# Near and strided values of a dilated head summed in the same two PSUM banks

## The chip, the cores and the metric

The kernel runs on one core of a Trainium2 chip. The metric is the device time of one execution in microseconds (us). The kernel before takes 1144.44 us as the median of 3 runs (1144.17 to 1147.55). Five engines take part: TensorE (PE in the profile; its weight loads are PEld), VectorE (DVE), ScalarE (ACT), GpSimd (POOL), and SyncE (SP), which issues the DMAs. Each engine runs its own instructions in order.

## The reference

Two layers of a decoder on 1024 tokens of width 1024, each with a pre-RMSNorm, a gate and a residual. Layer 1 is a latent attention that this change does not touch. Layer 0 has 8 sliding-window heads (A) and 8 dilated heads (B). A dilated head of 64 columns attends three times, with window and stride (128, 1), (512, 4) and (2048, 16); the three outputs are merged by the weights of their softmax denominators:

```python
for window, dil in B_CONFIGS:                      # (128,1), (512,4), (2048,16)
    bias_b, band_b = band_bias(rel_bias[:, A_HEADS:], dil, window // dil)
    o, lse = banded_attention(to_strided(qb, dil), to_strided(kb, dil), to_strided(vb, dil), bias_b, band_b)
    outs.append(from_strided(o, b, s, dil))
    lses.append(from_strided(lse, b, s, dil))
wts = jax.nn.softmax(jnp.stack(lses), axis=0)
ob = jnp.sum(wts[..., None] * jnp.stack(outs).astype(jnp.float32), axis=0)
...
return (o * jax.nn.silu(z)) @ w_out
```

## The kernel before, in words

Layer 0 makes the normed input transposed (`hH`, `hL`: a rounded part and the rest, since each product is made of reduced-precision matmuls), projects values, queries, keys and gates with `tproj`, runs 16 heads in 8 pairs (pairs 0 to 3 are dilated, 4 to 7 sliding), multiplies by the gate and projects out.

A projection (`tproj`, L144) gives 128 columns (a pair of heads) by 1024 tokens in two halves of 512 tokens; 24 matmuls of 512 columns make a half, and an evacuation takes the half out of its bank.

A dilated head (`head_b`, L530) has two sets of scores. The near scores (`banded`, L238) take 8 blocks of 128 queries against their own and the previous block of keys, in 4 parts; the strided scores (`s4`, L554) take the tokens of each residue mod 4 (the stride 16 is folded into the bias of the stride 4). `scores` (L216) runs two matmuls a region into a bank `sc` (two of them), DVE adds the bias and takes the row minimum (L227), ACT takes the exponential (L230). Keys lie by residue (the token 4j + r at r*256 + j). Queries lie in token order in `q`; a copy by residue, `q4`, is made by POOL after the second half of the projection (L470) and feeds the strided scores only.

The two sets have row statistics in different row orders; `to_tokens`, `merge` and `from_tokens` (L571 to L608) bring them together by small matmuls (L578, L604) with permutation matrices and give each row its factor, `fac`.

The values: POOL scales the rows of the score tiles (`scale_rows`, L235), PE transposes four 128 by 128 pieces into a bank, ACT and DVE take them out as `pth` and `ptl` (`transpose_split`, L183), and matmuls add values times these into banks tagged `ot`, of which there are two (L201). The near values (`banded_pv`, L254) go to two such banks in token order, key block by key block: two matmuls of up to 256 query columns for each. Each bank is taken out by `evac_sum` (L105): an ACT copy of one half of the partitions, a DVE add of the other (L108), into the tile `o`. Then the strided values (`pv4`, `pv4b`) take two banks again, in the order of residues; four DVE adds of 64 by 512 elements (L655) read them and add them into `o` at every fourth place:

```python
O4 = d["O"].rearrange("p (i r) -> p r i", r=4)
...
for half in (acc[g].ps[0:HD], acc[g].ps[HD:P]):
    V.tensor_tensor(dst, dst, half.rearrange("p (r i) -> p r i", r=2), op=ALU.add)
```

`finish` (L484) multiplies the gate by `o` on POOL and sends it to memory.

The order: the loop at L703 emits, for each head n, its near values beside the next head's scores, then its strided values beside the next head's statistics, then a projection to fill (queries and keys of the next pair after an even head, the pair's gate after an odd one). The kernel is built with a planner (`schedule_with_timeline_sim=True`) that simulates a timeline and sets each engine's order from it, so projections stand between the steps of the heads in the trace.

Of the kernel before, what the change touches and what calls it, by code (L numbers as in the profile page):

```python
# [10 lines left out]
F32 = mybir.dt.float32  # L11
F32R = mybir.dt.float32r
# [3 lines left out]
ALU = mybir.AluOpType  # L16
AX = mybir.AxisListType
# [3 lines left out]
SEQ = 1024  # L21
# [19 lines left out]
def f(ap):  # L41
    return ap.bitcast(F32)
# [152 lines left out]
class Acc:  # L195
# [2 lines left out]
        self.c, self.ps, self.first, self.parts = c, c.bank("ot", parts), None, parts  # L198

    def add(self, cols, lhsT, rhs, stop=False):  # L200
        m = self.c.mark = self.c.T.matmul(self.ps[:min(self.parts, lhsT.shape[-1]), cols], lhsT, rhs,  # L201
                                          start=self.first is None, stop=stop, skip_group_check=True)
        if self.first is None:
            self.first = m
        else:
            self.c.order(self.first, m)
# [83 lines left out]
def layer0(c, x, norm_w, rel_bias, w_in, w_out, onehot, band, perm, x1d, tables, before_out, x1_done):  # L290
# [86 lines left out]
    def tl(pool, shape, dt, tag, bufs):  # L377
        return pool.tile(shape, dt, name=tag, tag=tag, bufs=bufs)
# [1 line left out]
    pm = sp.tile([P, 4 * P + 312], F32, name="pm")  # L380
    dma.dma_start(pm, perm)

    S4, S4T = pm[:, P:2 * P], pm[:, 3 * P:4 * P]
    o = 4 * P
    in4, out4, sel, unsel = [pm[:, o + a:o + b] for a, b in ((8, 12), (20, 24), (24 + 128, 24 + 192), (24 + 192 + 64, 24 + 192 + 96))]

    def bias_tile(h, cfg, tag):
        b = tl(sp, [P, 256], F32, tag, 2)
        dma.dma_start(b, bass.AP(wr.tensor, wr.offset + (cfg * 16 + h) * P * 384 + 127, [[383, P], [1, 256]]))
        return b  # L390

    def q_evac(Qe, Qo):
        def evac(hf, ps, s):
            c.copy(Qe[0:HD, s], ps[0:HD], 0.125)
            c.copy(Qo[HD:P, s], ps[HD:P], 0.125)
            c.low(Qe[HD:P, s], ps[0:HD], Qe[0:HD, s], 0.125)
            c.low(Qo[0:HD, s], ps[HD:P], Qo[HD:P, s], 0.125)
# [54 lines left out]
    def proj_qk(pr):  # L452
        e = pairs[pr]
        b = pr < 4

        def alloc():
            e["q"] = [tl(qk, [P, SEQ], F32R, "q1", 3) for _ in range(2)]
            if b:
                e["q4"] = [tl(qk, [P, SEQ], F32R, "q4", 2) for _ in range(2)]
                e["k"] = [tl(qk, [P, SEQ], F32R, "kh", 3) for _ in range(2)]  # L460
                e["kl"] = [tl(qk, [P, SEQ], F32R, "kl", 3) for _ in range(2)]
            else:
                e["k"], e["kl"] = [A["k"][(pr - 4) // 2]] * 2, [A["kl"][(pr - 4) // 2]] * 2
        ev_k = lambda hf, ps, s: k_evac(*e["k"], *e["kl"], True)(hf, ps, s)

        def ev_q(hf, ps, s):
            q_evac(*e["q"])(hf, ps, s)
            if b and hf:
                for a, t in zip(e["q"], e["q4"]):
                    G.tensor_copy(t.rearrange("p (r j) -> p r j", r=R4), f(a).rearrange("p (j r) -> p r j", r=R4))  # L470
        out = [alloc]
        if b:
            out += tproj(c, hH, hL, w_in, B_COLS[1] + pr * P, ev_k) + [lambda: (dup(*e["k"]), dup(*e["kl"]))]
        return out + tproj(c, hH, hL, w_in, (B_COLS[0] + pr * P) if b else (pr - 4) * P, ev_q)
# [9 lines left out]
    def finish(pr):  # L484
        e = pairs[pr]
        eng = G if pr < 7 else V
        for hf in range(2):
            s = slice(hf * HALF, (hf + 1) * HALF)
            eng.tensor_tensor(e["gate"][:, s], e["gate"][:, s], e["o"][:, s], op=ALU.mult)
            if pr == 7:  # L490
                gH, gL = e["split"]
                c.copy(gH[:, s], e["gate"][:, s])
                c.low(gL[:, s], e["gate"][:, s], gH[:, s])
        if pr < 7:
            dma.dma_start(gd[pr], e["gate"])
# [34 lines left out]
    def head_b(pr, ei):  # L530
# [3 lines left out]
        p1, p4 = [], []  # L534

        def begin():
            nat = bias_tile(8 + h, 0, "b1")

            b1 = tl(sp, [P, 256], F32, "b1r", 2)
            G.tensor_copy(b1.rearrange("p (k r a) -> p k r a", k=2, r=R4), nat.rearrange("p (k a r) -> p k r a", k=2, r=R4))  # L540
            d["b4"] = bias_tile(8 + h, 1, "b4")

            N, L = d["nat"], d["own"] = tl(sp, [P, 2, 2, 8], F32, "nat", 2), tl(sp, [P, 2, 8], F32, "own", 2)
            k, kl = [e[n][ei].rearrange("p (r j) -> p r j", r=R4) for n in ("k", "kl")]
            d["t4"] = [e["q4"][ei].rearrange("p (r j) -> p r j", r=R4), k, kl]

            def keys(a, b):
                if b - a == 1:
                    return [t[:, :, a * RA:b * RA] for t in (k, kl)]
                return [e[n][ei].rearrange("p (r n a) -> p n r a", r=R4, a=RA)[:, a:b] for n in ("k", "kl")]  # L550
            d["parts"] = banded(c, p1, e["q"][ei], keys, b1, N[:, 0, 0], N[:, 0, 1], BIG)
            d["parts"][0]()

        def s4(r):  # L554
# [11 lines left out]
        def spread(out, vals, mask, vb, mb):  # L566

            shape = list(out.shape)
            V.tensor_tensor(out, vals.unsqueeze(vb).to_broadcast(shape), mask.unsqueeze(mb).to_broadcast(shape), op=ALU.mult)

        def to_tokens():  # L571
            N, L = d["nat"], d["own"]
            u = tl(sp, [P, 64], F32, "u", 1)
            for vh in range(4):
                spread(u[:, 16 * vh:16 + 16 * vh].rearrange("p (b r) -> p b r", r=4),
                       L.rearrange("p v (h r) -> p (v h) r", r=4)[:, vh], in4, 1, 2)
            ps = c.bank("pt")
# [21 lines left out]
        def from_tokens():  # L599
            fac, e = d["fac"], d["e"]  # L600
            u = tl(sp, [P, 64], F32, "u", 1)[:, :32]
            spread(u.rearrange("p (b r) -> p b r", r=4), e[:, 1], out4, 2, 1)
            ps = c.bank("pt")
            T.matmul(ps[:, 0:32], S4T, u, start=True, stop=True)  # L604
            x = tl(sp, [P, 64], F32, "x", 1)[:, :32]
            V.tensor_tensor(x, ps[:, 0:32], unsel, op=ALU.mult)
            V.tensor_reduce(fac[:, 1].rearrange("p (h r) -> p h r", h=2), x.rearrange("p (h b r) -> p h r b", h=2, r=4),
                            axis=AX.X, op=ALU.add)  # L608
# [11 lines left out]
            dma.dma_start(f(V4).rearrange("p (a b) d -> p a b d", b=2),  # L620
                          bass.AP(vd.tensor, vd.offset + h * P, [[4 * R_, P], [R_, 4], [HALF * R_, 2], [1, P]]))

        def evac(hf, acc):
            if hf == 0:
                d["O"] = out_rows(pr, lo)
            c.evac_sum(d["O"][:, hf * HALF:(hf + 1) * HALF], acc, lo)
        pv1 = banded_pv(c, p1, lambda: d["fac"][:, 0], lambda k: d["v"][0][:, k], evac)
        fc = lambda j: d["fac"][:, 1, j:j + 1]
        acc = []

        def pv4(g):
            if g == 0:
                acc.extend([Acc(c, P), Acc(c, P)])
            sl = []
            for r in (2 * g, 2 * g + 1):
                scale_rows(c, p4[r][:, 0:P], fc(r))
                scale_rows(c, p4[r][:, P:384], fc(4 + r))
                sl += [p4[r][:, 0:P], p4[r][:, P:256]]
            ph, pl = transpose_split(c, sl)
            for i in range(2):  # L640
                s = 2 * (2 * g + i)
                cc = slice(i * 256, (i + 1) * 256)
                pv2(acc[g], cc, d["v"][1][:, s], ph, pl, cc)

        def pv4b():
            O4 = d["O"].rearrange("p (i r) -> p r i", r=4)
            ph, pl = transpose_split(c, [p4[r][:, 256:384] for r in range(4)])
            for g in range(2):
                for i in range(2):
                    r = 2 * g + i  # L650
                    pv2(acc[g], slice(i * 256 + P, (i + 1) * 256), d["v"][1][:, 2 * r + 1], ph, pl,
                        slice(r * P, (r + 1) * P), i == 1)
                dst = O4[:, 2 * g:2 * g + 2]
                for half in (acc[g].ps[0:HD], acc[g].ps[HD:P]):
                    V.tensor_tensor(dst, dst, half.rearrange("p (r i) -> p r i", r=2), op=ALU.add)  # L655
# [717 lines left out]
```

## Time and profile before

| | |
|---|---|
| median of 3 runs | 1144.44 us |
| profiled execution | 1145.62 us, span 1143.8 us |
| busy over the span: PE, PEld | 1082.5 us (95%), 924.3 us (81%) |
| DVE, ACT, POOL | 695.2 us (61%), 589.4 us (52%), 504.5 us (44%) |
| mean granted TensorE clock | 0.974 of full speed |
| matmuls of L201 (both inputs) | 864 |
| POOL copies of q (L470) | 8, median 2034 ns |

Busy times are unions of the instructions' durations. A matmul's row has its latency, so the time that matmuls cost in a stream is read from start to start. PEclk is the granted clock as a share of 2.4 GHz; 0.50 is the lower level of 1.2 GHz. The name after `<-` in brackets is what ended the idle time before an instruction.

### The profile page before, as it was taken

How to read it: one execution, taken by the hardware profiler on the slowest of the kernel's cores; microseconds unless marked ns; L12 is line 12 of the kernel's file. 1: busy time of each engine (PE TensorE's matmuls, PEld its weight loads, DVE VectorE, ACT ScalarE, POOL GpSimd, SP SyncE). 2: the span in 40 equal slices, each digit the busy share in tenths (PEclk: the TensorE clock that was granted, in tenths of full speed). 3: DMA queues.
4: the chain of work that ended last, by engine and by line, in shares of the span. 5: the costliest groups of instructions: out<-in, count | busy, mean ns of one | idle time of the engine just before them, and what ended most of it. 6: DMA issues, size and time to landing. Idle time of an engine off the chain costs nothing.

```text
span 1143.8 us, 17221 instructions
## 1 busy us (share of the span) xinstructions
PE 1082.5 (95%) x5862; PEld 924.3 (81%) x5862; DVE 695.2 (61%) x1675; ACT 589.4 (52%) x1419; POOL 504.5 (44%) x535
## 2 busy tenths in 40 slices
PE   7998989899989999999999999999999999988997
PEld 4786778788878888778889988779888888777786
DVE  6534777557776665663331242678888898885333
ACT  5425545455555565653223232567777777685211
POOL 3113545445354344563113123275755665676301
PEclk9999989899999899989999999999999999999999
DMA  9948115142223221164322011132302311620312
GB/s 303 279 142 167 51 47 138 43 116 75 74 85 102 78 83 60 36 193 145 106 76 66 10 47 47 46 79 66 75 14 66 70 31 40 175 74 19 111 74 74
DMA packets 85975, 102.42 MB, mean 90 GB/s; under 512 B 6832, under 2 KB 69840, under 8 KB 85888
## 3 DMA queue, kind: packets, MB, share of 16 engines
q1 hardware_dynamic: 85888, 101.33, 31.6%
q8 instruction: 46, 0.75, 0.3%
q14 instruction: 41, 0.34, 0.1%
HBM read 67.97 MB, written 21.28 MB: 78 GB/s over the span
## 4 chain that ended last, share of the span: by engine, by line
PE 79%; DVE 8%; ACT 4%; DMA 4%; issue 3%; POOL 1%; SPq 0%; POOLq 0%; ACTq 0%; DVEq 0%
PE tp L116 14%; PE tp L118 14%; PE tp L117 14%; PE ot L201 8%; PE pt L188 7%; PE sc L1077 3%; PE sc L1078 2%; PE sc L1079 2%; PE ot L118 2%; PE sc L223 2%; PE ot L116 2%; PE ot L117 2%; PE sc L224 2%; PE pt L116 1%; PE pt L118 1%
## 5 line engine op out<-in xcount | busy, mean ns | idle before, releaser
L235 POOL TENSOR_TENSOR pc<-pc,ast 128x896 f32<-128x896 f32 (+7 forms) x128 | 145.6, 1155 | 114.6 <-DVE ast L1090 104.6
L116 PE MATMUL tp<-hH,wh 128*128 128x512 f32 x480 | 191.7, 400 | 0.6 <-ACT hH L96 0.3
L117 PE MATMUL tp<-hL,wh 128*128 128x512 f32 x480 | 190.5, 397 | 0.0
L118 PE MATMUL tp<-hH,wl 128*128 128x512 f32 x480 | 190.3, 397 | 0.0
L101 DVE TENSOR_TENSOR ptl<-pt,pth 128x512 fp32r<-128x512 f32 (+2 forms) x248 | 157.7, 643 | 40.2 <-ACT pth L96 36.1
L96 ACT ACTIVATE pth<-pt 128x512 fp32r<-128x512 f32 (+2 forms) x248 | 135.9, 562 | 75.3 <-PE pt L188 71.3
L111 POOL TENSOR_TENSOR wl<-wst,wh 128x512 fp32r<-128x512 f32 x60 | 78.3, 1309 | 146.6 <-ACT wh L96 124.8
L201 PE MATMUL ot<-pth,vt 128*128 128x256 f32 (+3 forms) x432 | 128.7, 313 | 12.4 <-ACT pth L96 5.1
L201 PE MATMUL ot<-ptl,vt 128*128 128x256 f32 (+3 forms) x432 | 116.8, 305 | 7.2 <-DVE ptl L101 6.9
L1088 ACT ACTIVATE pc<-sc,ast 128x896 f32<-128x896 f32 (+7 forms) x128 | 94.8, 741 | 28.9 <-DVE ast L1086 21.8
L116 PEld LDWEIGHTS tp<-hH,wh 128*128 128x128 f32 x480 | 91.5, 191 | 18.2 <-DVE kl L101 0.7
L118 PEld LDWEIGHTS tp<-hH,wl 128*128 128x128 f32 x480 | 91.3, 190 | 17.7
L1086 DVE CUSTOM_DVE_ANT_0 sc<-sc,mask 128x256 f32<-128x256 f32 (+7 forms) x128 | 97.3, 761 | 12.7 <-PE sc L1079 6.8
L117 PEld LDWEIGHTS tp<-hL,wh 128*128 128x128 f32 x480 | 91.4, 190 | 16.6
L201 PEld LDWEIGHTS ot<-pth,vt 128*128 128x128 f32 x432 | 83.6, 196 | 25.0 <-ACT pth L96 9.6
L188 PE MATMUL pt<-ident,pc 128*128 128x128 f32 x576 | 89.8, 277 | 1.0 <-POOL pc L235 0.9
L201 PEld LDWEIGHTS ot<-ptl,vt 128*128 128x128 f32 (+1 forms) x432 | 75.6, 179 | 17.3 <-DVE ptl L101 12.4
L235 POOL TENSOR_TENSOR p<-p,fac 128x256 f32<-128x256 f32 (+1 forms) x128 | 65.4, 549 | 48.1 <-DVE e L597 45.3
L1077 PE MATMUL sc<-kh,qh 96*128 96x384 f32 (+4 forms) x192 | 72.9, 380 | 4.6 <-ACT pc L1088 3.5
L188 PEld LDWEIGHTS pt<-ident,pc 128*128 128x128 f32 x576 | 68.2, 142 | 7.2 <-POOL pc L235 1.4
L96 ACT ACTIVATE wh<-wst 128x512 fp32r<-128x512 f32 x60 | 37.9, 632 | 58.3 <-PE tp L117 39.1
L1078 PE MATMUL sc<-kl,qh 96*128 96x384 f32 (+4 forms) x192 | 66.2, 345 | 1.7 <-DMA kl<-kd 1.7
(319 smaller groups left out, 2518.4 us busy)
## 6 DMA issues: line engine op xcount, KB each, us to landing
wst<-in_ab_w_in_dram SPq DMA_DIRECT2D x44, 256.0 KB, 3.1
kh<-kh SPq DMA_DIRECT2D x17, 256.0 KB, 3.1
kl<-kl SPq DMA_DIRECT2D x17, 256.0 KB, 4.2
xt<-in_x_dram SPq DMA_DIRECT2D x8, 512.0 KB, 5.8
vd<-vt SPq DMA_DIRECT2D x8, 512.0 KB, 3.8
vt<-vd SPq DMA_DIRECT2D x32, 128.0 KB, 3.1
vt<-vd SPq DMA_DIRECT2D x8, 512.0 KB, 5.0
xr<-in_x_dram SPq DMA_DIRECT2D x8, 512.0 KB, 4.0
```

The costliest lines, as they stand in the source:

```text
L96: return self.S.activation(out, in_, AF.Copy, scale=scale)
L101: return self.V.tensor_tensor(out, in_, f(high), op=ALU.subtract)
L116: m = self.order(after, self.order(prev, self.T.matmul(ps, lh, rh, start=start, stop=False)))
L117: m = self.order(m, self.T.matmul(ps, lh, rl, start=False, stop=False))
L118: return self.order(m, self.T.matmul(ps, ll, rh, start=False, stop=stop))
L188: c.T.transpose(ps[:, i * P:(i + 1) * P], s, c.ident)
L201: m = self.c.mark = self.c.T.matmul(self.ps[:min(self.parts, lhsT.shape[-1]), cols], lhsT, rhs, start=self.first is None, stop=stop, skip_ ...
L235: c.scaled = c.G.tensor_tensor(ap, ap, factor.to_broadcast(list(ap.shape)), op=ALU.mult)
L1077: m = c.order(m, T.matmul(o, qh[0:96, q], kh[0:96, k0:k1], start=True, stop=False))
L1078: m = c.order(m, T.matmul(o, qh[0:96, q], kl[0:96, k0:k1], start=False, stop=False))
L1086: V.tensor_tensor_reduce(out=ps, in0=ps, in1=mask[:, SEQ - n:], scale=-1.0, scalar=BIG, op0=ALU.add, op1=ALU.min, accum_out=neg)
L1088: S.activation(pt, ps, AF.Exp, bias=neg, scale=-1.0, accum_out=den)
```

## The change

The queries are evacuated by residue straight from PSUM into `q`, which now feeds the strided scores. POOL makes from it, after each half, the near queries `qn`: within each block of 128 tokens, by residue mod 4 and then by place (32 each). So rows of near scores stand in that order, the same one in which the near keys already were. The bias table of the near scores is loaded in four DMAs of 32 rows. The maps between the two row orders become one matrix, `same`. The near values are written by four matmuls a key block, each with an output of two runs (two residues, 64 or 32 columns each), into the two `ot` banks that the strided values then add to; these are taken out once, by `evac_sum`, at the end. `o` of a dilated pair lies by residue, and `finish` reads it and the gate accordingly.

```diff
+    def add_to(self, out, lhsT, rhs, stop=False):
+        m = self.c.mark = self.c.T.matmul(out, lhsT, rhs, start=self.first is None, stop=stop, skip_group_check=True)
...
-    S4, S4T = pm[:, P:2 * P], pm[:, 3 * P:4 * P]
+    same = sp.tile([P, R4, RA], F32, name="same")
+    V.tensor_reduce(same[:, 0], c.ident.rearrange("p (b a) -> p a b", a=RA), axis=AX.X, op=ALU.add)
+    V.tensor_copy(same[:, 1:], same[:, 0:1].to_broadcast([P, R4 - 1, RA]))
...
-    def bias_tile(h, cfg, tag):
+    def bias_tile(h, cfg, tag, quarters=False):
...
+        if quarters:
+            for r in range(R4):
+                dma.dma_start(b[r * RA:(r + 1) * RA], bass.AP(wr.tensor, o + 383 * r, [[4 * 383, RA], [1, 256]]))
...
-    def q_evac(Qe, Qo):
+    def q_evac(Qe, Qo, strided):
...
+            if strided:
+                e, o = [t.rearrange("p (r h j) -> p h r j", r=R4, h=2)[:, hf] for t in (Qe, Qo)]
+                ps = ps.rearrange("p (j r) -> p r j", r=R4)
...
-            q_evac(*e["q"])(hf, ps, s)
-            if b and hf:
-                for a, t in zip(e["q"], e["q4"]):
-                    G.tensor_copy(t.rearrange("p (r j) -> p r j", r=R4), f(a).rearrange("p (j r) -> p r j", r=R4))
+            q_evac(*e["q"], b)(hf, ps, s)
+            if b:
+                for a, t in zip(e["q"], e["qn"]):
+                    G.tensor_copy(t.rearrange("p (b r a) -> p r b a", r=R4, a=RA)[:, :, 4 * hf:4 * hf + 4],
+                                  f(a).rearrange("p (r b a) -> p r b a", r=R4, a=RA)[:, :, 4 * hf:4 * hf + 4])
...
+            if pr < 4:
+                g = e["gate"][:, s].rearrange("p (j r) -> p r j", r=R4)
+                eng.tensor_tensor(g, g, e["o"].rearrange("p (r h j) -> p h r j", r=R4, h=2)[:, hf], op=ALU.mult)
...
-            nat = bias_tile(8 + h, 0, "b1")
+            nat = bias_tile(8 + h, 0, "b1", True)
...
-            d["t4"] = [e["q4"][ei].rearrange("p (r j) -> p r j", r=R4), k, kl]
+            d["t4"] = [e["q"][ei].rearrange("p (r j) -> p r j", r=R4), k, kl]
...
-            d["parts"] = banded(c, p1, e["q"][ei], keys, b1, N[:, 0, 0], N[:, 0, 1], BIG)
+            d["parts"] = banded(c, p1, e["qn"][ei], keys, b1, N[:, 0, 0], N[:, 0, 1], BIG)
...
-            T.matmul(ps[:, 0:64], S4, u, start=True, stop=True)
+            T.matmul(ps[:, 0:64], same, u, start=True, stop=True)
...
-            T.matmul(ps[:, 0:32], S4T, u, start=True, stop=True)
+            T.matmul(ps[:, 0:32], same, u, start=True, stop=True)
...
-        def evac(hf, acc):
-            if hf == 0:
-                d["O"] = out_rows(pr, lo)
-            c.evac_sum(d["O"][:, hf * HALF:(hf + 1) * HALF], acc, lo)
-        pv1 = banded_pv(c, p1, lambda: d["fac"][:, 0], lambda k: d["v"][0][:, k], evac)
+        def near(b0, n, v, ph, pl, at):
+            for w, t in ((v, ph), (v[:, :HD], pl)):
+                t = t[:, at:at + n * P].rearrange("p (b r a) -> p r b a", b=n, r=R4)
+                for g in range(2):
+                    o = acc[g].ps.rearrange("p (r j) -> p r j", r=2)[:, :, b0 * RA:(b0 + n) * RA]
+                    acc[g].add_to(o[:w.shape[-1]], w, t[:, 2 * g:2 * g + 2])
...
+        def pv1(i):
+            k = 2 * i
+            if i == 0:
+                acc.extend([Acc(c, P), Acc(c, P)])
+                scale1(0)
+            for b in (k + 1, k + 2):
+                if b < NT:
+                    scale1(b)
+            ph, pl = transpose_split(c, [blk(k, k), blk(k + 1, k), blk(k + 1, k + 1)] + ([blk(k + 2, k + 1)] if k + 2 < NT else []))
+            v = d["v"][0]
+            near(k, 2, v[:, k], ph, pl, 0)
+            near(k + 1, 2 if k + 2 < NT else 1, v[:, k + 1], ph, pl, 256)
...
         def pv4(g):
-            if g == 0:
-                acc.extend([Acc(c, P), Acc(c, P)])
...
         def pv4b():
-            O4 = d["O"].rearrange("p (i r) -> p r i", r=4)
             ph, pl = transpose_split(c, [p4[r][:, 256:384] for r in range(4)])
+            O = out_rows(pr, lo)
             for g in range(2):
...
-                dst = O4[:, 2 * g:2 * g + 2]
-                for half in (acc[g].ps[0:HD], acc[g].ps[HD:P]):
-                    V.tensor_tensor(dst, dst, half.rearrange("p (r i) -> p r i", r=2), op=ALU.add)
+                c.evac_sum(O[:, g * HALF:(g + 1) * HALF], acc[g].ps, lo)
```

## Rows read from the trace of the kernel before

**Rows 1.** windows of the stage: length, busy us (x instructions) of PE, PEld, DVE, ACT, POOL; granted clock; DMA

```profile
130.00:150.00 20.00, 12.96 (x77) 11.24 (x77) 19.54 (x59) 11.56 (x41) 8.30 (x10) 0.82 0.29 80
...
200.00:214.00 14.00, 9.86 (x59) 8.47 (x58) 10.29 (x23) 4.95 (x12) 12.29 (x16) 0.90 0.31 81
...
214.00:320.00 106.00, 105.54 (x605) 91.56 (x605) 69.75 (x213) 56.31 (x168) 48.01 (x67) 0.98 0.28 73
...
380.00:400.00 20.00, 17.18 (x104) 15.67 (x103) 14.42 (x33) 12.48 (x36) 7.53 (x9) 0.83 0.29 86
```

**Rows 2.** windows again, three stretches at half the clock, same columns

```profile
146.30:156.50 10.20, 7.90 (x36) 7.63 (x37) 8.75 (x29) 5.98 (x23) 8.14 (x17) 0.50 0.17 46
211.20:217.90 6.70, 5.84 (x19) 4.85 (x19) 3.69 (x10) 2.42 (x9) 1.28 (x1) 0.50 0.01 2
388.70:395.40 6.70, 6.30 (x34) 6.12 (x32) 5.59 (x17) 4.71 (x14) 2.52 (x2) 0.50 0.30 103
```

**Rows 3.** groups by line and form, 84 to 400 us: busy, mean ns, idle before

```profile
L655 DVE TENSOR_TENSOR o<-o,ot 64x512 f32<-64x512 f32 x32 | 34.0, 1086 | 5.7 <-PE ot L201 5.1
...
L108 DVE TENSOR_TENSOR o<-ot,o 64x512 f32<-64x512 f32 x18 | 12.3, 685 | 4.6 <-ACT o L96 4.3
...
L103 DVE SCALAR_TENSOR_TENSOR q<-tp,q 64x512 fp32r<-64x512 f32 x24 | 16.5, 689 | 20.1 <-ACT q L96 19.7
...
L101 DVE TENSOR_TENSOR kl<-tp,kh 64x512 fp32r<-64x512 f32 x16 | 11.0, 687 | 7.5 <-ACT kh L96 7.2
...
L96 ACT ACTIVATE o<-ot 64x512 f32<-64x512 f32 x19 | 11.2, 592 | 13.2 <-PE ot L201 12.7
```

**Rows 4.** timeline of PE, place A: start, us, instruction, [idle before, releaser]

```profile
147.01 0.48 PE L223 MATMUL sc<-kh,q 128*128 128x128 f32 x1 [2.18 <-ACT p L230]
...
149.83 0.61 PE L604 MATMUL pt<-u,pm 128*128 128x32 f32 x2 [1.59 <-DVE u L569]
```

**Rows 5.** timeline of DVE, place A, same columns

```profile
143.39 2.06 DVE L655 TENSOR_TENSOR o<-o,ot 64x512 f32<-64x512 f32 x2
...
147.44 1.07 DVE L655 TENSOR_TENSOR o<-o,ot 64x512 f32<-64x512 f32 x1
```

**Rows 6.** timeline of all engines, place B

```profile
203.32 3.76 POOL L235 TENSOR_TENSOR p<-p,fac 128x128 f32<-128x128 f32 x8
...
206.66 1.08 DVE L655 TENSOR_TENSOR o<-o,ot 64x512 f32<-64x512 f32 x1
...
207.77 1.41 DVE L103 SCALAR_TENSOR_TENSOR q<-tp,q 64x512 fp32r<-64x512 f32 x2
...
208.52 3.97 POOL L470 CAST q<-q 128x1024 fp32r<-128x1024 f32 x2 [0.20 <-DVE q L103]
...
208.60 0.36 PE L223 MATMUL sc<-kh,q 128*128 128x256 f32 x1 [1.70 <-DVE q L103]
...
209.73 2.05 DVE L655 TENSOR_TENSOR o<-o,ot 64x512 f32<-64x512 f32 x2
...
211.93 0.44 PE L201 MATMUL ot<-pth,vt 128*128 128x128 f32 x1 [0.68 <-DVE o L655]
```

**Rows 7.** timeline of PE, place C

```profile
387.88 0.36 PE L201 MATMUL ot<-pth,vt 128*128 128x256 f32 x1 [1.78 <-DVE o L655]
388.07 0.28 PE L201 MATMUL ot<-ptl,vt 128*128 128x256 f32 x1
388.19 0.28 PE L201 MATMUL ot<-pth,vt 128*128 128x256 f32 x1
```

**Rows 8.** timeline of PE, the last strided values of a head

```profile
384.15 0.27 PE L201 MATMUL ot<-pth,vt 128*128 128x128 f32 x1
...
384.50 0.23 PE L201 MATMUL ot<-ptl,vt 128*64 128x128 f32 x1
```

**Rows 9.** groups by line and form, POOL, 84 to 400 us

```profile
L489 POOL TENSOR_TENSOR gate<-gate,o 128x512 f32<-128x512 f32 x8 | 10.1, 1288 | 7.2 <-DVE o L655 7.2
```

**Rows 10.** one line's instructions, the bias tables: ns min/median/max, first and last start

```profile
L389 SPq DMA_DIRECT2D b<-wr x24: 319/339/731, 47.0 to 443.6; - x24
```

More of the change, by code (lines that the diff above doesn't have):

```diff
@@ L200, in add @@
     def add(self, cols, lhsT, rhs, stop=False):
-        m = self.c.mark = self.c.T.matmul(self.ps[:min(self.parts, lhsT.shape[-1]), cols], lhsT, rhs,
-                                          start=self.first is None, stop=stop, skip_group_check=True)
+        self.add_to(self.ps[:min(self.parts, lhsT.shape[-1]), cols], lhsT, rhs, stop)
+    def add_to(self, out, lhsT, rhs, stop=False):
+        m = self.c.mark = self.c.T.matmul(out, lhsT, rhs, start=self.first is None, stop=stop, skip_group_check=True)
         if self.first is None:
@@ L381, in layer0 @@
     dma.dma_start(pm, perm)
-    S4, S4T = pm[:, P:2 * P], pm[:, 3 * P:4 * P]
     o = 4 * P
-    in4, out4, sel, unsel = [pm[:, o + a:o + b] for a, b in ((8, 12), (20, 24), (24 + 128, 24 + 192), (24 + 192 + 64, 24 + 192 + 96))]
-    def bias_tile(h, cfg, tag):
-        b = tl(sp, [P, 256], F32, tag, 2)
-        dma.dma_start(b, bass.AP(wr.tensor, wr.offset + (cfg * 16 + h) * P * 384 + 127, [[383, P], [1, 256]]))
+    quarter, unsel = pm[:, o + 8:o + 12], pm[:, o + 24 + 192 + 64:o + 24 + 192 + 96]
+    same = sp.tile([P, R4, RA], F32, name="same")
+    V.tensor_reduce(same[:, 0], c.ident.rearrange("p (b a) -> p a b", a=RA), axis=AX.X, op=ALU.add)
+    V.tensor_copy(same[:, 1:], same[:, 0:1].to_broadcast([P, R4 - 1, RA]))
+    same = same.rearrange("p r a -> p (r a)")
+    def bias_tile(h, cfg, tag, quarters=False):
+        b = tl(sp, [P, 256], F32, tag, 2)
+        o = wr.offset + (cfg * 16 + h) * P * 384 + 127
+        if quarters:
+            for r in range(R4):
+                dma.dma_start(b[r * RA:(r + 1) * RA], bass.AP(wr.tensor, o + 383 * r, [[4 * 383, RA], [1, 256]]))
+        else:
+            dma.dma_start(b, bass.AP(wr.tensor, o, [[383, P], [1, 256]]))
         return b
-    def q_evac(Qe, Qo):
+    def q_evac(Qe, Qo, strided):
         def evac(hf, ps, s):
[L394 to L397, printed above, removed]
+            e, o = Qe[:, s], Qo[:, s]
+            if strided:
+                e, o = [t.rearrange("p (r h j) -> p h r j", r=R4, h=2)[:, hf] for t in (Qe, Qo)]
+                ps = ps.rearrange("p (j r) -> p r j", r=R4)
+            c.copy(e[0:HD], ps[0:HD], 0.125)
+            c.copy(o[HD:P], ps[HD:P], 0.125)
+            c.low(e[HD:P], ps[0:HD], e[0:HD], 0.125)
+            c.low(o[0:HD], ps[HD:P], o[HD:P], 0.125)
         return evac
@@ L458, in alloc @@
             if b:
-                e["q4"] = [tl(qk, [P, SEQ], F32R, "q4", 2) for _ in range(2)]
+                e["qn"] = [tl(qk, [P, SEQ], F32R, "qn", 2) for _ in range(2)]
                 e["k"] = [tl(qk, [P, SEQ], F32R, "kh", 3) for _ in range(2)]
@@ L488, in finish @@
             s = slice(hf * HALF, (hf + 1) * HALF)
-            eng.tensor_tensor(e["gate"][:, s], e["gate"][:, s], e["o"][:, s], op=ALU.mult)
+            if pr < 4:
+                g = e["gate"][:, s].rearrange("p (j r) -> p r j", r=R4)
+                eng.tensor_tensor(g, g, e["o"].rearrange("p (r h j) -> p h r j", r=R4, h=2)[:, hf], op=ALU.mult)
+            else:
+                eng.tensor_tensor(e["gate"][:, s], e["gate"][:, s], e["o"][:, s], op=ALU.mult)
             if pr == 7:
@@ L575, in to_tokens @@
                 spread(u[:, 16 * vh:16 + 16 * vh].rearrange("p (b r) -> p b r", r=4),
-                       L.rearrange("p v (h r) -> p (v h) r", r=4)[:, vh], in4, 1, 2)
+                       L.rearrange("p v (h r) -> p (v h) r", r=4)[:, vh], quarter, 1, 2)
             ps = c.bank("pt")
-            T.matmul(ps[:, 0:64], S4, u, start=True, stop=True)
-            x = tl(sp, [P, 64], F32, "x", 1)
-            V.tensor_tensor(x, ps[:, 0:64], sel, op=ALU.mult)
-            V.tensor_reduce(N[:, 1].rearrange("p v b -> p (v b)"), x.rearrange("p (a r) -> p a r", r=4), axis=AX.X, op=ALU.add)
+            T.matmul(ps[:, 0:64], same, u, start=True, stop=True)
+            x = tl(sp, [P, 64], F32, "x", 1).rearrange("p (a r) -> p a r", r=4)
+            V.tensor_tensor(x, ps[:, 0:64].rearrange("p (a r) -> p a r", r=4), quarter.unsqueeze(1).to_broadcast([P, 16, 4]),
+                            op=ALU.mult)
+            V.tensor_reduce(N[:, 1].rearrange("p v b -> p (v b)"), x, axis=AX.X, op=ALU.add)
         def merge():
@@ L601, in from_tokens @@
             u = tl(sp, [P, 64], F32, "u", 1)[:, :32]
-            spread(u.rearrange("p (b r) -> p b r", r=4), e[:, 1], out4, 2, 1)
+            spread(u.rearrange("p (b r) -> p b r", r=4), e[:, 1], quarter, 2, 1)
             ps = c.bank("pt")
-            T.matmul(ps[:, 0:32], S4T, u, start=True, stop=True)
+            T.matmul(ps[:, 0:32], same, u, start=True, stop=True)
             x = tl(sp, [P, 64], F32, "x", 1)[:, :32]
@@ L621, in load_v, with blk, scale1 @@
                           bass.AP(vd.tensor, vd.offset + h * P, [[4 * R_, P], [R_, 4], [HALF * R_, 2], [1, P]]))
-        def evac(hf, acc):
-            if hf == 0:
-                d["O"] = out_rows(pr, lo)
-            c.evac_sum(d["O"][:, hf * HALF:(hf + 1) * HALF], acc, lo)
-        pv1 = banded_pv(c, p1, lambda: d["fac"][:, 0], lambda k: d["v"][0][:, k], evac)
+        acc = []
+        def near(b0, n, v, ph, pl, at):
[4 more added lines that the diff above has]
+                    acc[g].add_to(o[:w.shape[-1]], w, t[:, 2 * g:2 * g + 2])
+        def blk(q, k):
+            o = (q % 2) * 256 + (P if q == k else 0)
+            return p1[q // 2][:, o:o + P]
+        def scale1(b):
+            o = (b % 2) * 256
+            scale_rows(c, p1[b // 2][:, o + (0 if b else P):o + 256], d["fac"][:, 0, b:b + 1])
+        def pv1(i):
[10 more added lines that the diff above has]
+            near(k + 1, 2 if k + 2 < NT else 1, v[:, k + 1], ph, pl, 256)
         fc = lambda j: d["fac"][:, 1, j:j + 1]
-        acc = []
         def pv4(g):
-            if g == 0:
-                acc.extend([Acc(c, P), Acc(c, P)])
             sl = []
@@ L652, in pv4b @@
                         slice(r * P, (r + 1) * P), i == 1)
-                dst = O4[:, 2 * g:2 * g + 2]
-                for half in (acc[g].ps[0:HD], acc[g].ps[HD:P]):
-                    V.tensor_tensor(dst, dst, half.rearrange("p (r i) -> p r i", r=2), op=ALU.add)
-        pv = [load_v] + pv1 + [lambda: pv4(0), lambda: pv4(1), pv4b]
+                c.evac_sum(O[:, g * HALF:(g + 1) * HALF], acc[g].ps, lo)
+        pv = [load_v] + [lambda i=i: pv1(i) for i in range(4)] + [lambda: pv4(0), lambda: pv4(1), pv4b]
         return sc, pv, [to_tokens, merge, from_tokens]
```

## The prediction

> **What bounds the kernel now.** I read the busy shares stretch by stretch first, then the gaps of TensorE in order of time, then what released each gap. The change touches only the dilated heads, which run from about 88 to 400 us; layer 1 and the sliding heads keep their work. In most of that stretch TensorE (PE) is the bound: from 214 to 320 us it is busy 105.54 of 106.00 us while VectorE (DVE) is busy 69.75. Three places are different [rows 1]. From 130 to 150 DVE is busy 19.54 of 20 us and PE only 12.96. From 200 to 214 PE is idle 4.1 us of 14, and from 380 to 400 2.8 us of 20. Behind each of the three PE is granted only 1.2 GHz for a while; the busy PE time in those stretches is 7.90, 5.84 and 6.30 us [rows 2], and half of each (3.9, 2.9, 3.1) would come back at 2.4 GHz. So DVE work taken away is worth something in three places of one head each; in the other five heads it goes from beside a full PE and is worth nothing, while PE work added there counts in full.
>
> **The change, part by part.**
>
> *The four adds at the end of a head go.* L655 is 32 adds of 1.086 us, four a head, 34 us of DVE [rows 3]. Their worth is read in the three places.
> Place A, 143 to 150: PE stands 2.18 us before a score matmul and 1.59 us before L604 [rows 4]. DVE runs two L655 (2.06 us) ahead of the score step behind the first gap, and one of 1.07 us ahead of the step behind the second [rows 5]. Four adds are 4.3 us; the two sums of the evacuation (L108, 0.685 us each [rows 3]) now stand there, 1.4 us, and their old places earlier in the head come free on a DVE that is as full. Removed in all 4.3, of which I take 3.0, since short waits on other engines take over.
> Place B, 205 to 213: one L655 (1.08 us) starts at 206.66 ahead of the q evacuation L103, which starts at 207.77 and releases PE's score at 208.60 after 1.70 us idle. Two more (2.05 us) at 209.73 hold the `ot` bank, for which PE waits 0.68 us [rows 6]. Of 4.1 us idle I take 3.0 (1.1 before the q evacuation, 1.9 behind).
> Place C: PE waits 1.78 us on L655 for a bank [rows 7]. The new release is an ACT copy (0.592) and an L108 (0.685), 1.28 us, against two L655, 2.17 us [rows 3]: 0.9, taken as 0.8.
> The clock: stretches at 1.2 GHz cost 3.9, 2.9 and 3.1 us. Each starts in or just behind a gap that shrinks but does not vanish, so I take half, half and a third: 2.0, 1.5 and 1.0.
> Gain: 3.0 + 3.0 + 0.8 + 4.5 = 11.3 us. Bounds: 0, and with all PE idle of the three places (7.0 + 4.1 + 2.8) and all clock (9.9) 23.8.
>
> *The near values cost more PE instructions.* Before, a near key block is two matmuls of 256 columns, 0.12 us from start to start [rows 7]. After, it is four of 128 columns: two with 128 weight columns and two with 64. The trace has that mix in pv4b: from 384.15 to 384.50 four matmuls, two of each weight width, take 0.35 us [rows 8]; the 128-column ones don't go below about 0.11, so halving the moving columns does not halve the step. Blocks 0, 1, 2, 4, 5 and 6 go from 0.24 to 0.35 us (6 x 0.11 = 0.66); block 3 has four matmuls before and after; block 7 goes from two to four (0.17 more). That is 0.83 us a head and 6.6 us over eight heads. In the gap places (two heads of eight) idle PE hides it: 5.0. Bounds 3 and 6.6.
> The new outputs lie in PSUM as two runs, and no row has such an output. Nearest are contiguous outputs of the same column count [rows 8]: below, no change (the columns are as many, so a gain has no source); above, each takes what two 256-column steps take, 0.24 instead of 0.0875, for 256 matmuls 39 us. I take no change, being nearest to a row of equal size. For a strided PSUM read the trace speaks: the k evacuation on DVE reads PSUM at stride four and takes 0.687 us, the q evacuation reads it contiguously and takes 0.689 [rows 3], so the new strided q evacuation is priced at nothing. The Trainium skill's page "SBUF — State Buffer", in its section on Door 1 (the DMA port swizzle), says that any non-contiguous PSUM pattern slows matmuls significantly; for reads by DVE this trace shows no such thing, for matmul outputs no run here shows either. By that sentence the sum would turn positive (the fourth rival).
>
> *The near scores now wait for POOL's copy of q.* Before, POOL's 2.0 us copies fed only the strided scores, later. After, the near queries are that copy: per half, two casts of half the size, 1.0 us each by half of 3.97/2 [rows 6]. Blocks 0 to 3 need the first half, which is evacuated half a projection (24 matmuls of 512 columns) earlier, so that copy is hidden. Blocks 4 to 7 of the first head of each pair need DVE's evacuation, POOL's queue and one cast. Behind the waiting score matmul PE has values of the other head and projections; at 208.60 nothing else was ready, so there it counts. Bounds: 0 (the strided scores lose the same wait), and for four pairs the cast (1.0) plus a run of eight row scalings ahead of it in POOL's order (3.76 [rows 6]), 19 us. I take 1.0, at place B.
>
> *At nothing:* the evacuation moved behind the strided values (same two copies and two sums; the wait for banks in the middle of a head goes, the next head's first values now need both banks, free about 0.59 + 2 x 0.685 = 2.0 us after the last matmul, as against 2.2 us for its first bank before); the gate product with strided views (POOL, 1.29 us each [rows 9]; at the DVE ratio of strided to plain adds, 1.086/0.685, it would be 2.0, 6 us over eight, on an engine busy 48 of 106 us beside PE); the bias table in four DMAs (24 more issues of 0.34 us on SP [rows 10], 8 us over 300, asked for a head ahead; bound 0 to 2 if a weight load queues behind them at a gap); the `same` matrix (two small DVE operations once).
>
> **Sum.** 5.0 + 1.0 - 11.3 = -5.3 us. The profiled execution took 1145.62 us (span 1143.8 and 1.8 around it): 1140.3. The median of the runs is 1.2 us lower, 1144.44, so I give 1139.
>
> **The rivals.**
> 1. *Everything returns:* all PE idle of the three places and all clock, 23.8, less 6.6 and 1.0: -16, 1128. For it: from 130 to 150 DVE is the only full engine. Against: the scores there are also a chain of PE, DVE and ACT with two banks, and other gaps than those of L655 stand in it.
> 2. *The loads eat the gain:* the gaps shrink (6.8 us) but the clock still falls, and the added PE time counts everywhere: 6.6 + 1.0 - 6.8 = +0.8, 1145. For it: five of eight heads have PE full. Against: two of the three stretches at 1.2 GHz begin inside gaps that L655 makes.
> 3. *Slower, by POOL's copy:* at the starts of the second to fourth pair the scores of blocks 4 to 7 wait for casts behind row scalings. Two such starts at 2.5 us idle and 3.4 us of lost clock each, 11.8, in place of the 1.0: +5.5, 1150. It is slower than before once the starts cost over 6.3 us together. For it: POOL runs in order, and its cast at 208.52 started only 0.2 us after it could [rows 6], with 3.76 us of scalings just before. Against: only half a head hangs on it, and where PE has projections they fill in.
> 4. *Two-run outputs are slow:* +39 us, 1178. For it: nothing in the trace. Against: moving operands with runs of 32 elements are already fed to the near scores.
>
> **How the numbers follow.** A measurement here tells a change from none at about 0.3%, 3.4 us. Chances: forecast 0.44, rival 1 0.12, rival 2 0.22, rival 3 0.18, rival 4 0.04. So faster 0.56, same 0.22, slower 0.22. The forecast's own range is 1134 to 1141; the range that leaves out no more than 2 in 10 goes from 1131 (into rival 1) to 1150 (rival 3).
>
> **What would show it.** After: no line with adds from `ot` beside the evacuation; DVE busy about 34 us less and PE's matmul count up by 14 a head, 112; the mix of four near matmuls at 0.35 us (over 0.45: rival 4); PE idle between 130 and 150 down from 7.0 to about 4; fewer or shorter stretches at 1.2 GHz before 400 us (unchanged: rival 2); a score matmul that waits for POOL's cast at a pair's start (over 2 us at two pairs: rival 3). I am wrong if the planner, which sets each engine's order anew, puts the freed DVE time where PE is full, or moves the start of layer 1's work by more than these sums.

## The result, and the profile after

The changed kernel takes 1137.84 us as the median of seven runs, the kernel before 1144.17 on the same chip: a ratio of 0.9941, with its 95% interval in brackets [0.9914, 0.9969], 6.3 us less. The prediction was 1139. The profiled execution took 1138.69 us, its span is 6.9 us shorter than before.

The head of the page after (busy time, share of the span, instructions):

```profile
span 1136.9 us, 17458 instructions
...
PE 1083.2 (95%) x5974; PEld 923.6 (81%) x5974; DVE 662.3 (58%) x1645; ACT 589.3 (52%) x1419; POOL 499.2 (44%) x543
```

DVE is busy 32.9 us less than the 695.2 of before, PE 0.7 us more.

The windows of [rows 1], now after, with one more at 320 (length; busy us and instructions of PE, PEld, DVE, ACT, POOL; granted clock; DMA):

```profile
130.00:150.00 20.00, 16.66 (x100) 15.43 (x98) 14.82 (x58) 12.34 (x44) 9.27 (x18) 0.74 0.38 93
...
200.00:214.00 14.00, 11.45 (x62) 9.52 (x61) 8.68 (x24) 7.22 (x17) 10.99 (x20) 0.76 0.28 77
...
214.00:320.00 106.00, 106.00 (x664) 93.28 (x664) 59.59 (x216) 58.99 (x180) 49.34 (x70) 1.00 0.31 87
...
320.00:340.00 20.00, 19.45 (x119) 16.50 (x118) 11.23 (x33) 10.06 (x25) 10.70 (x18) 1.00 0.31 82
...
380.00:400.00 20.00, 20.00 (x123) 17.64 (x122) 12.66 (x33) 13.21 (x35) 10.54 (x16) 1.00 0.31 93
```

PE's idle time, against [rows 1], goes from 7.0 to 3.3 us in place A, from 4.1 to 2.6 in B, from 2.8 to nothing in C. The window at 320, in which the prediction saw no place, gives 2.6 us, nearly as much as place C: before it was

```profile
320.00:340.00 20.00, 16.81 (x104) 14.91 (x103) 14.40 (x47) 12.34 (x38) 7.73 (x10) 0.94 0.37 119
```

and its gaps were a wait for a DMA and one for the statistics, not for L655 (timeline of PE, before):

```profile
326.54 0.39 PE L201 MATMUL ot<-pth,vt 128*128 128x256 f32 x1 [1.38 <-DMA kh<-in_ab_w_out_dram]
...
337.48 0.60 PE L604 MATMUL pt<-u,pm 128*128 128x32 f32 x2 [1.81 <-DVE u L569]
```

The stretches at the lower clock, 88 to 500 us, as windows after:

```profile
108.30:115.10 6.80, 4.83 (x16) 3.84 (x16) 5.48 (x19) 3.29 (x13) 0.00 (x0) 0.50 0.72 166
132.20:142.40 10.20, 10.20 (x54) 10.17 (x55) 6.87 (x28) 5.15 (x20) 3.15 (x5) 0.50 0.21 57
207.30:214.10 6.80, 6.13 (x22) 4.97 (x22) 3.15 (x5) 3.14 (x8) 4.52 (x10) 0.50 0.42 116
473.50:487.20 13.70, 9.85 (x29) 7.08 (x28) 13.59 (x13) 8.66 (x17) 11.69 (x7) 0.50 0.27 71
```

and those of before that are not in [rows 2]:

```profile
108.70:115.50 6.80, 5.35 (x15) 4.38 (x16) 4.41 (x14) 3.09 (x13) 0.00 (x0) 0.50 0.56 140
132.60:136.00 3.40, 3.40 (x19) 3.40 (x19) 3.37 (x8) 3.25 (x11) 3.40 (x2) 0.51 0.42 116
...
337.40:340.80 3.40, 3.32 (x14) 3.25 (x15) 3.04 (x7) 0.00 (x0) 3.40 (x7) 0.51 0.29 77
...
487.60:494.40 6.80, 5.10 (x14) 3.54 (x12) 6.57 (x6) 5.64 (x11) 6.80 (x4) 0.50 0.19 50
```

Half of the busy PE time in them is what the clock costs at most. Up to 400 us it falls from 16.1 to 10.6. But a longer stretch, 13.7 us for 6.8, lies around the start of the output projection. That projection's first matmul starts 11.1 us earlier than before (478.06 against 489.14), and it then waits for its split operands (timeline of PE, after):

```profile
478.06 0.80 PE L116 MATMUL tp<-woh,gh 128*128 128x512 f32 x1 [0.60 <-ACT gh L96]
...
482.42 0.79 PE L118 MATMUL tp<-woh,gl 128*128 128x512 f32 x1 [2.07 <-DVE gl L101]
```

The projection ends 6.6 us earlier: 586.6 to 580.0. From 88 us to that end, before and after:

```profile
88.00:586.60 498.60, 471.45 (x2586) 405.57 (x2585) 304.26 (x802) 252.14 (x685) 224.62 (x284) 0.96 0.33 92
```
```profile
88.00:580.00 492.00, 474.53 (x2703) 407.98 (x2702) 269.89 (x771) 251.73 (x685) 219.24 (x292) 0.96 0.34 94
```

So nearly the whole gain lies here: idle PE falls by 9.7 us (27.2 to 17.5), busy PE rises by 3.1. This window (length, busy, and their difference) is the yardstick of the experiments.

### The profile page after: what moved, and what is told of

It is laid out like the page before. It is cut to its first block, busy times and chain, and to the rows that moved or that the text cites. A ratio compares the mean times of both kernels' runs of the same rounds, so it can differ in the third digit from the quotient of the medians.

```text
span 1136.9 us, 17458 instructions
## 1 busy us (share of the span) xinstructions
PE 1083.2 (95%) x5974; PEld 923.6 (81%) x5974; DVE 662.3 (58%) x1645; ACT 589.3 (52%) x1419; POOL 499.2 (44%) x543
## 4 chain that ended last, share of the span: by engine, by line
PE 79%; DVE 6%; ACT 5%; DMA 5%; issue 3%; POOL 1%; SPq 0%; POOLq 0%; ACTq 0%; DVEq 0%
PE tp L116 14%; PE tp L118 14%; PE tp L117 14%; PE ot L204 8%; PE pt L188 7%; PE sc L1123 3%; PE sc L1124 2%; PE sc L1125 2%; PE sc L225 2%; PE ot L118 2%; PE ot L116 2%; PE ot L117 2%; PE sc L226 2%; PE pt L116 1%; PE pt L118 1%
## 5 line engine op out<-in xcount | busy, mean ns | idle before, releaser
L204 PE MATMUL ot<-pth,vt 128*128 128x128 f32 (+2 forms) x488 | 133.9, 307 | 7.3 <-ACT pth L96 6.0
L204 PE MATMUL ot<-ptl,vt 128*64 128x128 f32 (+2 forms) x488 | 118.6, 288 | 4.9 <-DVE ptl L101 4.7
L204 PEld LDWEIGHTS ot<-pth,vt 128*128 128x128 f32 x488 | 90.6, 196 | 19.9 <-ACT pth L96 10.0
L204 PEld LDWEIGHTS ot<-ptl,vt 128*128 128x128 f32 (+1 forms) x488 | 78.3, 170 | 15.1 <-DVE ptl L101 8.7
```

What stands on the lines that cost most here:

```text
L204: m = self.c.mark = self.c.T.matmul(out, lhsT, rhs, start=self.first is None, stop=stop, skip_group_check=True)
```

## The experiments

The prediction's theory: the four adds held PE in three places, and their removal outweighs the dearer near values. A first rival: the price of those is another than was worked out. When pe_price came out faster than before, a second had to be weighed: the planner's order is different, and another order of the same work moves the time as much. Each ratio is to the kernel before on the same chip, and a point is one per cent of the time before.

**The price alone: pe_price.** The kernel before, with its near values in the change's matmul shapes but contiguous outputs; all adds stay.

```diff
+            h = n // 2
+            for w, t in ((v(k), ph), (v(k)[:, :HD], pl)):
+                for i in range(2):
+                    a.add(slice(q0 + i * h, q0 + i * h + h), w, t[:, at + i * h:at + i * h + h], ...)
```

> The kernel before, with one thing of the change: each near step of a dilated head that took two matmuls of 256 columns takes four of 128 (two with 128 weight columns, two with 64), and block 7 four of 64. 112 matmuls more, the adds L655 as before. Theory (the added PE time counts, less what the two gap places hide): +5.0 us, 3 to 6.6, so 1149. Rival (the loads eat the gain): +6.6 or more, with longer stretches at 1.2 GHz beside. Rival (the added matmuls lie in PE's idle time): 0 to +2.

1139.23 us, 0.9962 [0.9948, 0.9975]: 4.4 us faster, with more work and nothing taken away. The matmuls did get dearer. Three near steps in a row after (timeline of PE; `x2` is two matmuls):

```profile
218.04 0.39 PE L204 MATMUL ot<-pth,vt 128*128 128x128 f32 x2
218.26 0.29 PE L204 MATMUL ot<-ptl,vt 128*64 128x128 f32 x2
218.39 0.38 PE L204 MATMUL ot<-pth,vt 128*128 128x128 f32 x2
218.61 0.29 PE L204 MATMUL ot<-ptl,vt 128*64 128x128 f32 x2
218.74 0.38 PE L204 MATMUL ot<-pth,vt 128*128 128x128 f32 x2
218.96 0.28 PE L204 MATMUL ot<-ptl,vt 128*64 128x128 f32 x2
219.08 0.95 PE L188 MATMUL pt<-ident,p 128*128 128x128 f32 x7
```

and a step of pe_price, to the transposes behind it:

```profile
222.25 0.38 PE L201 MATMUL ot<-pth,vt 128*128 128x128 f32 x2
222.47 0.28 PE L201 MATMUL ot<-ptl,vt 128*64 128x128 f32 x2
222.59 0.63 PE L188 MATMUL pt<-ident,p 128*128 128x128 f32 x4
```

0.35, 0.35 and 0.34 us with outputs in two runs, 0.34 with contiguous ones, 0.24 before. So the price of a step is as worked out, and the first rival falls; and yet PE's idle time is 10.1 us less than before, with the adds in place:

```profile
88.00:579.20 491.20, 474.10 (x2698) 407.69 (x2697) 304.26 (x802) 252.41 (x685) 223.49 (x284) 0.96 0.34 93
```

**The adds alone: no_adds and plain_adds.** The first is the kernel before without its four adds; the second lets them write consecutive places.

```diff
-                    V.tensor_tensor(dst, dst, half.rearrange("p (r i) -> p r i", r=2), op=ALU.add)
```

> The kernel before without the four adds L655 of each dilated head; the strided values are computed but stay out of the output. Theory (the adds are worth 11.3 us: 3.0 + 3.0 + 0.8 of idle PE time and 4.5 of clock, and here the evacuation is not moved, so up to 1.4 us more at the first place): -11 to -13 us, 1132. Rival (the gaps shrink but the clock still falls): -6 to -8, 1137. Rival (all idle time of the three places and all clock return): -20 or more.

> The kernel before with the four adds L655 writing contiguous columns of the same tile instead of every fourth one; the places of the strided values in the output are wrong. If an add costs what L108 costs (0.685 instead of 1.086 us), 0.4 x 32 = 12.8 us of VectorE go. Theory (the adds' length in the three places is what counts, 11.3 us for 4.3 us a head): about a third of it, -3 to -5 us, 1140. Rival (it is the two banks shared, which let PE go on from near to strided values without an evacuation between, that gives the gain): 0 to -1.

no_adds: 1128.19, 0.9863 [0.9842, 0.9883], 15 us. plain_adds: 1140.48, 0.9967 [0.9954, 0.998], 3 us; an add takes 0.684 us there instead of 1.086. The first gains more than the theory's 11 to 13 us, the second what it said. But beside pe_price, where nothing was taken away and 4.4 us were gained, this shows little. In no_adds the banks of the strided values also come free without being read, which no full kernel can have.

**The change again: after_again.**

> The changed kernel once more, beside the others on the same chip. 1138, a ratio to the kernel before of 0.991 to 0.997. By the theory the sum of the effects of the two kernels that do one half each (the PE price, +5; no adds, -11 to -13) less 1 for the q copy, and with 1.4 us at the first place for the moved evacuation: -4 to -7.

1138.24, 0.9948 [0.9928, 0.9968].

**The same work in another order: before_swap and after_swap.** In both, the loop emits the next head's statistics ahead of the strided values instead of behind.

```diff
-        interleave(marked(c, pv[5:], marks), rest)
+        interleave(rest, marked(c, pv[5:], marks))
```

> The kernel before with the same instructions, emitted in another order at one point: of the next head's three statistics steps and this head's three strided value steps, which alternate, the statistics step now comes first. The planner makes a new order from it. Theory (the adds L655 make the idle time of PE, 27.2 us between 88 and 587 us before, 17.5 in the changed kernel): 1144 within 2, idle time 25 to 29 us. Rival (the order that the planner happened on for the kernel before left 10 us of idle time that any other order would not, as the kernel with more matmuls and all adds suggests, with 17.1 us idle): -4 to -7, 1138 to 1140, idle time 17 to 20 us.

> The changed kernel with the same exchange in the order of emission. Theory: 1138 within 2 and idle time near 17.5 us. Rival (orders move the time by 4 us either way): 1134 to 1142, with no tie to the adds.

before_swap: 1139.5, 0.9967 [0.9956, 0.9979]; not one instruction's work is different, and it is 3.7 us faster, as the rival had it (the idle time, 22.2 us, lies between the two). after_swap: 1137.46, 0.9957 [0.9941, 0.9974].

**A second order: before_rev, after_rev and before_both.** The two scalings of a near step are emitted in reverse, in the sliding heads too, which share that code; before_both has both edits.

```diff
-            for b in (k + 1, k + 2):
+            for b in (k + 2, k + 1):
```

> The kernel before with another change of order alone: the two row scalings of a near step are emitted last block first. If the time of the kernel before in its own order is an outlier among its orders: 1138 to 1141, as with the statistics step first (0.9967). If that was a good draw and the first order is typical: 1142 to 1146.

> The changed kernel with the row scalings emitted last block first. With its own order (0.9948) and the other (0.9957) a third draw of the changed work. If the change is worth 2 to 3 us whatever the order (adds worth 4 us once the order is good, less 2 for PE): 1136 to 1139, below the mean of the orders of the kernel before by 2 to 4. If the gain was the order's: 1138 to 1142.

> The kernel before with both changes of order (statistics step first, row scalings last block first). Outlier: 1138 to 1141. Typical: 1142 to 1146. With the two others and the kernel itself this gives four orders of the same work.

before_rev: 1134.2, 0.9933 [0.9909, 0.9957]. before_both: 1135.69, 0.9939 [0.9917, 0.9961]. after_rev: 1134.0, 0.9925 [0.9904, 0.9946]. All three are faster than any reading had expected. Order by order, from the windows to the end of the output projection (idle is length less busy; granted clock):

| order | before: ratio | idle, busy PE, clock | after: ratio | idle, busy PE, clock |
|---|---|---|---|---|
| own | 1 | 27.2, 471.5, 0.96 | 0.9948 | 17.5, 474.5, 0.96 |
| swap | 0.9967 | 22.2, 467.7, 0.97 | 0.9957 | 18.2, 470.0, 0.98 |
| rev | 0.9933 | 21.5, 465.5, 0.96 | 0.9925 | 16.8, 470.1, 0.97 |
| both | 0.9939 | 24.8, 463.1, 0.98 | not run | |

In its own order the change is worth 0.52 points; in the two others 0.10 and 0.08, with intervals of about 0.2 and 0.3 on either side (the two intervals' halves, root of the sum of squares), so there it can't be told from nothing. Of the four orders of the kernel before its own is the slowest. The order works on more than idle time: with the same matmuls PE is busy 3.7 to 8.3 us less in the three others. The pairs have the same edit, not the same order, since the planner makes a new order for each kernel. In before_rev all 32 adds are there, and its windows at 320 and 380 are nearly full, as they are after the change:

```profile
320.00:340.00 20.00, 19.43 (x118) 16.77 (x118) 15.18 (x50) 12.76 (x37) 11.54 (x21) 1.00 0.51 141
380.00:400.00 20.00, 20.00 (x125) 17.80 (x124) 12.97 (x37) 13.42 (x37) 12.96 (x20) 1.00 0.25 87
```

The waits of PE on the adds, 88 to 400 us (in total, times, longest), before:

```profile
PE ot L201 <- DVE o L655: 2.5, 2, 1.8
```

In before_swap there is one such wait,

```profile
PE ot L201 <- DVE o L655: 0.5, 1, 0.5
```

and in before_rev none. So the second rival holds, as far as three pairs can tell: most of the gain in the kernel's own order is the order.

**Price without adds: price_no_adds.** Both edits of the first two experiments, to see the price where no add can hide it.

> The kernel before with four 128-column matmuls a near step and without the adds L655 (the strided values stay out of the output). By sums of the two halves alone (0.9962 and 0.9863 of the kernel before): 1124. By the theory that PE time counts in full once no idle time is left to hide it: 6.5 us over the kernel without adds, 1135. By the rival that the planner's order gave the gain of the kernel with more matmuls: the same 1135, and the adds are then worth only 4 to 5 us to a kernel with a good order.

1129.66, 0.9885 [0.9871, 0.9898], 0.22 points (2.5 us, with an interval of about as much on either side) above no_adds: neither the 1124 of the sum nor the 1135 of the two other readings. Against pe_price the adds are worth 0.77 points, 8.8 us. Its near matmuls have the change's shapes, and a head has as many evacuations; it is 0.63 points, 7 us, faster than after_again. That difference holds what the change does on top (both banks held from the near to the end of the strided values, the copies of q, the bias table in four), the strided banks that nothing reads here, and the order.

**Other banks: half_banks and half_swap.** The change with its two banks split by halves of the tokens instead of by residues: a near step is again two matmuls of 256 columns, with four runs each in the output; the strided values take 16 matmuls of 128 columns instead of 8 of 256; the first bank is complete, and taken out, one step ahead of the head's end. A head then has 42 of these matmuls instead of 48. half_swap has the order of before_swap too.

```diff
-                for g in range(2):
-                    o = acc[g].ps.rearrange("p (r j) -> p r j", r=2)[:, :, b0 * RA:(b0 + n) * RA]
-                    acc[g].add_to(o[:w.shape[-1]], w, t[:, 2 * g:2 * g + 2])
+                b = b0 % 4
+                o = acc[b0 // 4].ps.rearrange("p (r j) -> p r j", r=R4)[:, :, b * RA:(b + n) * RA]
+                acc[b0 // 4].add_to(o[:w.shape[-1]], w, t)
...
+            if g:
+                d["O"] = out_rows(pr, lo)
+                c.evac_sum(d["O"][:, :HALF], acc[0].ps, lo)
```

> The changed kernel with the two banks divided by the half of the tokens in place of the residues: a near step is again two matmuls of 256 columns (an output of four runs of 64), and the first part of the strided values takes 16 matmuls of 128 columns a head in place of 8 of 256; bank 0 is complete, and taken out, before the last strided step. 6 matmuls less a head; by 0.24 and 0.35 us for two and four matmuls a head takes 0.39 us less of PE, 3.1 us in all. Theory (PE is full beside the heads, so PE time counts): 1135, -3 against the changed kernel. Rival (the order decides): within 4 us of 1138 either way. If outputs of four runs were slow: +5 or more.

> The kernel with the banks divided by the half of the tokens (0.9902 in its own order), with the statistics step emitted first. If its lead of 5 us on the changed kernel comes from its PE work, 3.1 us less, and from the earlier free bank: 1130 to 1135 again. If it is a draw of the order: 1135 to 1140.

half_banks: 1132.16, 0.9902 [0.9888, 0.9917]. half_swap: 1127.77, 0.9866 [0.9842, 0.989], the fastest of the kernels that do all the work. Against the change in the same order they gain 0.46 and 0.91 points, 5 and 10 us, beyond the intervals in both orders, and half_swap is faster than both of its readings had it. half_banks in the window of the yardstick:

```profile
88.00:570.40 482.40, 466.86 (x2655) 401.45 (x2654) 268.43 (x772) 252.19 (x685) 217.88 (x292) 0.97 0.35 95
```

Against after, PE is busy 7.7 us less (3.1 by the estimate for the matmuls) and idle 1.9 us less. How much of it is the smaller matmul work, how much the earlier bank and how much again the order was not separated.

## Why the prediction was right, and where not

The time was right, 1139 for 1137.84. The reason was so only in part, and luck had a share.

**The step that failed: "Gain: 3.0 + 3.0 + 0.8 + 4.5 = 11.3 us".** It read three gaps of one order and took them for a property of the work. What came back in the kernel's own order is 9.7 us of idle PE; with the order varied alike on both sides, 4.0 (swap) and 4.7 (rev). The working named the planner as a way to be wrong and gave it no price; two edits that change no work moved the kernel before by 3.7 and 7.8 us. PE's busy time rises by 2.3 (swap) and 4.6 us (rev), so the change is worth near 1 us in those orders, which is inside its interval. That is the outcome of rival 2, the loads eat the gain; its clause that no clock comes back does not hold there (granted clock 0.97 to 0.98 and 0.96 to 0.97).

*Place A* was sized well: 3.7 us of idle time for 3.0. The two sums of the evacuation stand where the prediction put them: the first ahead of the step L592 that ends PE's gap of 1.65 us, the second just behind it (timeline of DVE, and then of PE, after):

```profile
145.97 0.67 DVE L108 TENSOR_TENSOR o<-ot,o 64x512 f32<-64x512 f32 x1
146.57 0.19 DVE L592 TENSOR_TENSOR u<-e,pm 128x32 f32<-128x32 f32 x1
146.68 0.68 DVE L108 TENSOR_TENSOR o<-ot,o 64x512 f32<-64x512 f32 x1
```
```profile
146.90 0.38 PE L628 MATMUL pt<-u,same 128*128 128x32 f32 x2 [1.65 <-DVE u L592]
...
150.05 0.33 PE L225 MATMUL sc<-kh,q 128*128 128x128 f32 x1 [0.74 <-ACT p L232]
```

In rev the idle time there also falls, from 6.8 to 3.1 us, in swap only from 3.2 to 2.8. *Place B* gave 1.6 us for 3.0: a wait for L630, the statistics, took the place of the wait for q:

```profile
205.71 0.63 PE L188 MATMUL pt<-ident,p 128*128 128x128 f32 x4 [1.61 <-DVE x L630]
```

*Place C* went altogether, 2.8 us for 0.8, but the adds need not go for that: before_swap, before_rev and pe_price have no idle time there with the adds in place. *The clock*: 4.5 taken; 5.5 came back up to 400 us, which is luck in the parts. By half of the busy time at the lower clock, place A gives 0.5 for 2.0 (10.20 us for 3.40 and 7.90), place B loses 0.1 for 1.5 (6.13 for 5.84), and place C gives 3.2 for 1.0; the other 1.9 come from 108 and 337 us, where no gain was taken. And 2.4 were lost again around the start of the output projection (half of 9.85 against half of 5.10), a stage outside the stretch that the prediction looked at. In before_swap, before_rev and before_both the lower clock lasts 10.2 us there for 6.8 in its own order, so this stretch differs with the order too.

**PE's price** was right: the mix at 0.35 us and 112 matmuls more. PE's busy time rises by 3.1 us net of some 3.1 that the clock gives back in the rows above, together 6.2, near the 6.6 of the sum before the deduction for gaps. By the Trainium skill's page "TensorE: Matmul & The Clock Gate", section LDWEIGHTS (loading the stationary operand), a load takes its column count over 1.2 in ns, by which an estimate for 128 and 64 columns is 107 and 53. The rows above agree, with about 0.11 and 0.06 us from start to start.

**Outputs in two runs** cost nothing: steps with runs of 64 columns are in the fences of after and pe_price, and block 7, with runs of 32, takes about 0.31 us in after (264.79 to 265.10) and as long with contiguous outputs in pe_price (264.33 to 264.63). Outputs in four runs of 64 cost nothing either. Four 256-column matmuls of half_banks, from 251.68 to 252.16, take 0.12 us each, as contiguous ones did [rows 7]:

```profile
251.68 0.28 PE L204 MATMUL ot<-pth,vt 128*128 128x256 f32 x1
251.79 0.28 PE L204 MATMUL ot<-ptl,vt 128*128 128x256 f32 x1
251.92 0.28 PE L204 MATMUL ot<-pth,vt 128*128 128x256 f32 x1
252.04 0.28 PE L204 MATMUL ot<-ptl,vt 128*128 128x256 f32 x1
252.16 0.23 PE L204 MATMUL ot<-pth,vt 128*128 128x128 f32 x1
```

Rival 4 falls, and with it, for runs of 32 and more fp32 columns, the sentence of the Trainium skill's page "SBUF — State Buffer" (section Door 1: The DMA port swizzle) that any non-contiguous PSUM pattern slows matmuls significantly.

**POOL's copy** was priced at 1.0 us, and no cost shows: no wait of PE from 88 to 400 us ends with it, so rival 3 falls. The cast was sized wrongly too, 0.62 us for 1.0. From the groups of after by form (busy, mean ns, idle before):

```profile
L103 DVE SCALAR_TENSOR_TENSOR q<-tp,q 64x512 fp32r<-64x512 f32 x26 | 17.9, 688 | 22.7 <-ACT q L96 22.2
...
L108 DVE TENSOR_TENSOR o<-ot,o 64x512 f32<-64x512 f32 x20 | 13.6, 686 | 3.7 <-ACT o L96 3.5
L510 POOL TENSOR_TENSOR gate<-gate,o 128x512 f32<-128x512 f32 x8 | 12.3, 1562 | 1.9 <-DVE o L108 1.9
...
L487 POOL CAST qn<-q 128x512 fp32r<-128x512 f32 x16 | 9.7, 617 | 14.6 <-DVE q L103 14.4
```

**At nothing**: the strided evacuation of q (688 ns for the 689 of [rows 3]) and the gate (1562 ns for 1288, inside its bound) were. The move of the evacuation behind the strided values may not have been: the 0.63 points between price_no_adds and the change, and the gain of half_banks, which frees a bank earlier, could come from the banks that are held longer. That is argued, not shown: a kernel with the change's matmuls and only the earlier bank was not run. The trace of after speaks rather against it: no wait of PE from 88 to 400 us ends with an evacuation of an `ot` bank. And of the 9.0 us by which the window of after_again (491.5 us) is longer than that of price_no_adds (482.5), 5.3 are busy PE on as many matmuls, at a granted clock of 0.96 for 0.98.

## What to carry to other kernels

Where a planner sets the order anew, a change of under one per cent is compared with two or three other orders of the same work, on both sides, before its gain is put down to its mechanism; here the order alone was worth up to 7.8 us, and the change itself, in the two other orders, about 1, which is inside the noise. A gap that is read in one order is priced by asking whether it survives a different order. Where two layouts share banks, a cut by which one bank is complete early and the moving operands stay wide is worth trying: the cut by token halves ran 5 and 10 us faster than the cut by residue, though which of its parts did it was not separated.

## What the runs showed of the hardware

POOL's cast that reads every fourth fp32 took 1.99 ns an element of a partition's row (2034 ns for 1024), the one that reads runs of 32 took 1.20 (617 for 512), 40% less. The Trainium skill's page "GPSIMD Engine Reference", section "Performance pitfalls for Q7 kernels", gives reads at a stride over 8 bytes 50% more time; the two casts are apart by 65%. DVE's evacuation of q did not change when it came to read PSUM at every fourth place and to write runs of 128 (688 against 689 ns). DVE's add into `o` did: 1086 ns where it reads and writes every fourth fp32 of `o`, 684 ns in plain_adds with consecutive places.
